# Output projection of three blocks inside the hand-ordered phase, a second column order, and delayed transposes

## The chip, the cores and the metric

The kernel runs on one core of one Trainium2 chip. The metric is device time in microseconds, the median of several executions of the same program. Engines are named as the profile names them: PE is TensorE's matmul side and PEld its weight loads, DVE is VectorE, ACT is ScalarE, POOL is GpSimd, and SP is SyncE, which issues all DMAs here.

## What is computed

One decoder layer on 2048 rows of 1024 columns, in float32. The rows are normed and multiplied by one input matrix. Its columns feed two groups of heads: eight heads of a delta-rule recurrence (RWKV-7) and four of a gated linear attention (GLA). Their outputs side by side, `mix`, go through one output matrix and are added to the input; a SwiGLU FFN and a last norm follow.

```python
n = rms_norm(h, rms1_g[l])
z = n @ w_in[l]
y_rwkv = rwkv7_mixer(z[..., :D_RWKV_IN], ...)
y_gla = gla_mixer(z[..., D_RWKV_IN:], ...)
mix = jnp.concatenate([y_rwkv, y_gla], axis=-1)
h = h + mix @ w_out[l]
n = rms_norm(h, rms2_g[l])
h = h + (silu(n @ ffn_gate[l]) * (n @ ffn_up[l])) @ ffn_down[l]
return rms_norm(h, final_g)
```

## The kernel before

Large products are done with three matmuls each: both operands are split into a high part (a cast on ACT) and a low part (a subtraction on DVE or POOL), and high x high, high x low and low x high are summed in one PSUM bank.

**Phase A** (`phase_a`, lines 326 to 388) computes the input product and the mixers in four blocks of 512 rows. Its instructions are put in order by `Order` (lines 66 to 242). Each `stream` is a generator that issues instructions and yields; `Order.run` keeps a modelled time for each and always resumes the earliest. A stream may yield nothing, the name of an event that it waits for, or a `set`, a `lock` or an `unlock`. A stream that is marked as filler is resumed when the modelled PE has less than 400 ns of work ahead. What comes out is a fixed order on each engine; an instruction whose input is late holds up all behind it on its engine.

The streams (`streams`, line 412):

- `zmm` (597), the filler: 26 columns of 128 outputs per block in the order SEQZ, 24 matmuls each, into banks zd0 and zd1 in turn. Its input tiles "nh" and "nl" (four each) hold the normed rows of a block.
- `weights` (569) loads each column's weights through two buffers "w_raw", casts them on ACT and subtracts on POOL, two columns ahead. `evac` (625) takes the columns out of the banks. `rows` (496) and `prep_a` (534) make the next block's nh and nl, with transposes on PE; two of eight use the bank "mg" and its lock.
- `stage_a` (797), `stage_a2` (938) and `stage_b` (1034) handle pairs of heads ("head" below), 16 in turn. `stage_a2` inverts a triangular system in a loop on POOL (966 to 971), transposes it twice on DVE (984, 986), and then PE runs zt (994) and more, up to wtp (1027). `stage_b` runs the recurrence in eight steps, norms the result on DVE (1092 to 1095), transposes it on PE (ytp, 1102) and stores it to `mix` in DRAM (1119).
- `gmix` (1123), the GLA heads: norm on DVE (1200), then the transpose gotp (1205) on PE, with "mg" locked.

**Phase B** (`phase_b`, 1251) is ordered by the framework, which fills the engines' free places with it while phase A ends. It splits the output matrix (1295), and for each of 16 row tiles loads `mix` and the residual, does 2 x 24 matmuls of 512 columns (1315 to 1317), adds, squares and stores `hs` (1318 to 1321). `prep` (1263) reads hs back, scales and transposes it for the FFN. Then comes the FFN in two halves of 1024 rows (1329 on).

Tiles of phase B take the buffers of phase A by lists of tags (`SEQ`, 1220, and `bt`, 1235): each call takes the next tag of its list. The list "raw" is bk (one buffer), br, br (four buffers); row tiles, residual tiles, the tiles of `prep` and raw FFN weights all draw from it.

Of the kernel before, what the change touches and what calls it, by code (L numbers as in the profile page):

```python
# [20 lines left out]
D = 1024  # L21
# [3 lines left out]
BLK = 512  # L25
# [40 lines left out]
class Order:  # L66
# [126 lines left out]
    def run(self, streams):  # L193

        q = [[0.0, n, name, gen, filler] for n, (name, gen, filler) in enumerate(streams)]
        waiting = {}
        while q:
            pe = self.free.get("PE", 0.0)
            s = min(q, key=lambda s: (max(s[0], pe - self.AHEAD) if s[4] else s[0], s[1]))
            q.remove(s)  # L200
            try:
                r = next(s[3])
            except StopIteration:
                self.take()
# [36 lines left out]
        assert not waiting, waiting.keys()  # L241
        self.check()
# [24 lines left out]
class K:  # L267
# [15 lines left out]

    def rsqrt(self, x, n, name):

        nc = self.nc
        y = self.small.tile([128, n], F32, name=name + "_y")
        t = self.small.tile([128, n], F32, name=name + "_t")
        nc.vector.tensor_scalar(out=y.bitcast(I32), in0=x.bitcast(I32), scalar1=-0.5, scalar2=float(0x5F3759DF),
                                op0=ALU.mult, op1=ALU.add)  # L290
# [4 lines left out]
        return y  # L295


    S2 = -0.5 ** (1 / 3)
# [27 lines left out]
    def phase_a(self, ctx):  # L326
        tc, nc, I = self.tc, self.nc, self.I
        self.ca = ca = ctx.enter_context(tc.tile_pool(name="ca", bufs=1))
        self.s = ctx.enter_context(tc.tile_pool(name="s", bufs=2))
        self.pp = ctx.enter_context(tc.tile_pool(name="pp", bufs=1, space=PSUM))  # L330
        self.x0 = []
        for k in range(KT):
            x = self.s.tile([128, NPR, 128], F32, name="xk", **self.X0[k])
# [56 lines left out]
    def stacks(self):  # L390
        nc = self.nc

        def stack(name, n, order):
# [15 lines left out]
    SEQZ = [ZL, ZK, ZR, ZV, ZQ, ZKG, ZVG, ZK + 1, ZR + 1, ZV + 1, ZVG + 1, ZG, ZOG, ZK + 2, ZR + 2, ZV + 2, ZOG + 1,  # L409
            ZQ + 1, ZKG + 1, ZK + 3, ZR + 3, ZV + 3, ZVG + 2, ZVG + 3, ZOG + 2, ZOG + 3]  # L410

    def streams(self):
        nb = self.T // BLK
        def each(f, m):
            for b in range(nb):
                for i in range(m):
                    yield from f(b, i)
        return [("b", each(self.stage_b, HP), False), ("a2", each(self.stage_a2, HP), False),
                ("e", self.evac(nb), False), ("w", self.weights(nb), False), ("x", self.rows(nb), False), ("p", self.prep_a(nb, 0), False), ("p", self.prep_a(nb, 1), False),
                
                ("a", each(self.stage_a, HP), False), ("g", each(self.gmix, 2), False),
                ("z", self.zmm(nb), True)]
# [146 lines left out]
    def weights(self, nb):  # L569
# [55 lines left out]
    def evac(self, nb):  # L625

        todo = {ZL: self.lora_l, ZG: self.lora_g}
        for b in range(nb):
            for i, ct in enumerate(self.SEQZ):
                if ct == ZQ or ct == ZQ + 1:  # L630
                    yield from self.decay_g(b, ct - ZQ)
                yield f"zm{b}.{i}"
                ps = self.zps.pop((b, i))
                used = ("set", f"ze{b}.{i}")
                if ct == ZL:
                    yield from self.lora_l(b, ps, used)
                elif ct == ZG:
                    yield from self.lora_g(b, ps, used)
                elif ct < ZL:
                    yield from self.rkv_z(b, ct, ps, used)  # L640
                else:
                    yield from self.gla_z(b, ct, ps, used)

    def shift(self, ps, i, rows=128):

# [105 lines left out]
    def gla_z(self, b, ct, ps, used):  # L751
# [32 lines left out]
        else:  # L784
# [7 lines left out]
            self.gla[i, h] = so  # L792
            yield used
            yield ("set", f"go{i}.{h}")


    def stage_a(self, b, hp):
# [140 lines left out]
    def stage_a2(self, b, hp):  # L938
# [95 lines left out]
    def stage_b(self, b, hp):  # L1034
# [11 lines left out]
        for c in range(NCH):  # L1046
# [26 lines left out]
            if c % 4 == 3:  # L1073
# [7 lines left out]
                for x in range(2):  # L1081
# [41 lines left out]
    def gmix(self, b, jj):  # L1123
# [44 lines left out]
        for h in range(2):  # L1168
# [19 lines left out]
            if h:  # L1188
# [46 lines left out]
    def bt(self, cls, name, shape, dtype=F32):  # L1235
        seq = self.SEQ[cls]
        i = self.nb_[cls] = self.nb_.get(cls, -1) + 1
        tag, bufs = seq[i % len(seq)]
        return (self.pp if cls in ("dn", "up") else self.s).tile(shape, dtype, name=name, tag=tag, bufs=bufs)

    def split(self, src, name, cls="W"):
        nc = self.nc
# [8 lines left out]
    def phase_b(self):  # L1251
# [7 lines left out]
        hs = self.dram.tile([T, D], F32, name="hs")  # L1259
        rs, n2 = {}, {}  # L1260
        rsb = self.base.tile([128, T // 128], F32, name="rsb")

# [29 lines left out]
                    n2[nb, k] = (h, l)  # L1292


        wo = [self.split(I["wout"][k * 128:(k + 1) * 128, :], "wo", "W" if k < 6 else "W2") for k in range(KT)]
        steps = [(nb, kp) for nb in range(NB) for kp in range(KT // 2)]
        for t in range(T // 128):
            raw = self.bt("raw", "raw", [128, KT, 128])
            nc.sync.dma_start(out=raw, in_=self.mix[t])
            mh, ml = [], []  # L1300
            for i in range(2):
# [2 lines left out]
                ml.append(self.bt("hid", "ml", [128, 4, 128], F32R))  # L1304
                nc.scalar.copy(out=mh[i], in_=a)
                nc.vector.tensor_tensor(out=ml[i], in0=a, in1=mh[i].bitcast(F32), op=ALU.subtract)
            h = self.bt("raw", "hx", [128, D])
            nc.sync.dma_start(out=h, in_=I["x"][t * 128:(t + 1) * 128, :])
            ss = self.small.tile([128, 2], F32, name="rn_ss")
            for d in range(2):  # L1310
                ps = self.pp.tile([128, 512], F32, name="op", tag=f"zd{d}", bufs=1)
                ds = slice(d * 512, d * 512 + 512)
                for k in range(KT):
                    a, l = mh[k // 4][:, k % 4, :], ml[k // 4][:, k % 4, :]
                    nc.tensor.matmul(out=ps, lhsT=a, rhs=wo[k][0][:, ds], start=(k == 0), stop=False)  # L1315
                    nc.tensor.matmul(out=ps, lhsT=a, rhs=wo[k][1][:, ds], start=False, stop=False)  # L1316
                    nc.tensor.matmul(out=ps, lhsT=l, rhs=wo[k][0][:, ds], start=False, stop=(k == KT - 1))  # L1317
                nc.vector.tensor_tensor(out=h[:, ds], in0=ps, in1=h[:, ds], op=ALU.add)
                nc.scalar.activation(out=self.bt("act", "sq", [128, 512]), in_=h[:, ds], func=AF.Square,
                                     accum_out=ss[:, d:d + 1])  # L1320
            nc.sync.dma_start(out=hs[t * 128:(t + 1) * 128, :], in_=h)
            rs[t] = self.row_rs(ss, rsb[:, t:t + 1])
# [152 lines left out]
```

## Time and profile before

| | us |
|---|---|
| median of 3 runs | 2888.27 (2887.42 to 2889.42) |
| profiled execution | 2882.94 |
| its span | 2881.1 |
| PE busy | 2736.8 (95%) |
| DVE busy | 1414.5 (49%) |
| ACT busy | 985.9 (34%) |
| POOL busy | 676.2 (23%) |
| DMA, mean over the span | 72 GB/s |

The profile is one execution. Busy time is the time in which an engine works on at least one instruction. The granted clock of PE is given as a share of full speed: 1.0 is 2.4 GHz, 0.5 is 1.2 GHz. Idle time of an engine is put down to what ended it. Phase A ends at about 1228 us, the loop of the output projection at about 1386 us; the rest is the FFN.

### The profile page before, as it was taken

Reading aid. Unit: us, or ns where it says so; the run is one execution under the profiler, and the core shown is the slowest. Engines: PE = TensorE matmul, PEld = TensorE weight load, DVE = VectorE, ACT = ScalarE, POOL = GpSimd, SP = SyncE. Lnnn points to the kernel's source line nnn. Section 1 sums busy time; section 2 is a strip of 40 time slices with the busy share of each in tenths; the row PEclk is TensorE's granted clock in tenths of the full one; section 3 lists DMA queues with packets and bytes.
Section 4 is the critical chain, followed back from the end, with each engine's and each line's share of the span. In section 5 each row is a group of like instructions: output and inputs, shape, how many; then the busy total and the mean of one; then the engine's idle time right before and its main releaser. Section 6 shows DMA issues by size and latency. Waiting matters only on the chain.

```text
span 2881.1 us, 38490 instructions
## 1 busy us (share of the span) xinstructions
PE 2736.8 (95%) x14856; PEld 2203.4 (76%) x14856; DVE 1414.5 (49%) x2938; ACT 985.9 (34%) x1907; POOL 676.2 (23%) x1458
## 2 busy tenths in 40 slices
PE   6898999999989998799999999999999999999998
PEld 4777777777767776588788888888878888888886
DVE  5466667676666665644333333333373333333334
ACT  7455554665555554333211111111151111111112
POOL 3666466556654665100000000000000000000000
PEclk9999999999999998799999999999999999999999
DMA  4122212231122111355411111111161111111111
GB/s 141 59 69 65 92 63 63 63 103 62 57 63 60 59 59 37 121 179 179 132 51 44 44 45 58 44 44 44 51 212 51 52 52 52 52 44 44 44 44 59
DMA packets 109641, 206.06 MB, mean 72 GB/s; under 512 B 9104, under 2 KB 50800, under 8 KB 109456
## 3 DMA queue, kind: packets, MB, share of 16 engines
q1 hardware_dynamic: 109456, 203.59, 22.4%
q8 instruction: 117, 1.92, 0.3%
q14 instruction: 68, 0.56, 0.1%
HBM read 178.39 MB, written 25.17 MB: 71 GB/s over the span
## 4 chain that ended last, share of the span: by engine, by line
PE 77%; DVE 9%; POOL 5%; ACT 4%; issue 3%; DMA 1%; SPq 0%; DVEq 0%; POOLq 0%; ACTq 0%
PE ups L1346 6%; PE ups L1348 6%; PE ups L1347 6%; PE dn L1369 6%; PE gps L1346 6%; PE dn L1368 6%; PE gps L1348 6%; PE gps L1347 5%; PE dn L1370 5%; PE zd L615 4%; PE zd L617 3%; PE zd L616 3%; PE op L1315 2%; PE op L1316 2%; PE op L1317 2%
## 5 line engine op out<-in xcount | busy, mean ns | idle before, releaser
L615 PE MATMUL zd<-nh,w_hi 128*128 128x512 f32 x832 | 360.3, 433 | 3.7 <-DVE k L657 2.0
L617 PE MATMUL zd<-nh,w_lo 128*128 128x512 f32 x832 | 333.8, 401 | 3.3 <-POOL w_lo L592 3.3
L616 PE MATMUL zd<-nl,w_hi 128*128 128x512 f32 x832 | 331.7, 399 | 1.2 <-DVE nl L562 1.2
L592 POOL TENSOR_TENSOR w_lo<-w_raw,w_hi 128x512 fp32r<-128x512 f32 x208 | 279.5, 1346 | 220.6 <-ACT w_hi L590 174.9
L1371 DVE TENSOR_TENSOR h<-dn,h 128x512 f32<-128x512 f32 x352 | 242.9, 690 | 179.8 <-PE dn L1370 179.7
L1369 PE MATMUL dn<-wdl,hh 128*128 128x512 f32 x704 | 278.6, 396 | 0.0
L1368 PE MATMUL dn<-wdh,hh 128*128 128x512 f32 x704 | 277.6, 395 | 0.0
L1370 PE MATMUL dn<-wdh,hl 128*128 128x512 f32 x704 | 277.0, 393 | 0.0
L1346 PE MATMUL ups<-n2h,wuh 128*128 128x512 f32 x660 | 260.4, 395 | 0.0
L1347 PE MATMUL ups<-n2l,wuh 128*128 128x512 f32 x660 | 260.4, 395 | 0.0
L1348 PE MATMUL ups<-n2h,wul 128*128 128x512 f32 x660 | 260.0, 394 | 0.0
L1347 PE MATMUL gps<-n2l,wgh 128*128 128x512 f32 x660 | 259.9, 394 | 0.0
L1346 PE MATMUL gps<-n2h,wgh 128*128 128x512 f32 x660 | 259.9, 394 | 0.0
L1348 PE MATMUL gps<-n2h,wgl 128*128 128x512 f32 x660 | 259.3, 393 | 0.0
L1351 DVE TENSOR_TENSOR sgu<-sgu,ups 128x512 f32<-128x512 f32 x88 | 60.2, 685 | 395.0 <-PE ups L1348 393.5
L1247 ACT CAST wdh<-raw 128x1024 fp32r<-128x1024 f32 x44 | 46.3, 1052 | 465.3 <-PE dn L1370 250.3
L617 PEld LDWEIGHTS zd<-nh,w_lo 128*128 128x128 f32 x832 | 159.7, 192 | 42.6 <-POOL w_lo L592 5.8
L615 PEld LDWEIGHTS zd<-nh,w_hi 128*128 128x128 f32 x832 | 160.7, 193 | 36.1 <-issue 5.1
L971 POOL TENSOR_TENSOR lm<-lm,lt 128x60 f32<-128x60 f32 (+24 forms) x496 | 174.6, 352 | 38.8
L616 PEld LDWEIGHTS zd<-nl,w_hi 128*128 128x128 f32 x832 | 161.2, 194 | 27.0 <-DVE nl L562 2.1
L969 POOL TENSOR_TENSOR lt<-lm,ln 128x60 f32<-128x60 f32 (+24 forms) x496 | 161.9, 326 | 38.1 <-DVE ln L953 13.8
L1350 ACT ACTIVATE sgu<-gps 128x512 f32<-128x512 f32 x88 | 52.7, 599 | 344.7 <-PE gps L1348 344.7
(265 smaller groups left out, 4967.7 us busy)
## 6 DMA issues: line engine op xcount, KB each, us to landing
w_raw<-in_win SPq DMA_DIRECT2D x208, 256.0 KB, 2.6
raw<-in_wg SPq DMA_DIRECT2D x44, 512.0 KB, 4.1
raw<-in_wu SPq DMA_DIRECT2D x44, 512.0 KB, 3.6
raw<-in_wd SPq DMA_DIRECT2D x44, 512.0 KB, 3.5
xk<-in_x SPq DMA_DIRECT2D x32, 256.0 KB, 3.3
hx<-in_x SPq DMA_DIRECT2D x16, 512.0 KB, 4.3
raw<-mix SPq DMA_DIRECT2D x16, 512.0 KB, 3.5
hs<-hx SPq DMA_DIRECT2D x16, 512.0 KB, 2.9
```

The source lines that it names most:

```text
L592: nc.gpsimd.tensor_tensor(out=wlo[:, ks, :], in0=raw, in1=whi[:, ks, :].bitcast(F32), op=ALU.subtract)
L615: nc.tensor.matmul(out=ps, lhsT=whi[:, k, :], rhs=nh, start=(k == 0), stop=False)
L616: nc.tensor.matmul(out=ps, lhsT=whi[:, k, :], rhs=nl, start=False, stop=False)
L617: nc.tensor.matmul(out=ps, lhsT=wlo[:, k, :], rhs=nh, start=False, stop=(k == KT - 1))
L971: nc.gpsimd.tensor_tensor(out=lm[:, 0:j, i0:], in0=lm[:, 0:j, i0:], in1=lt[:, 0:j, i0:], op=ALU.add)
L1346: nc.tensor.matmul(out=ps, lhsT=w[0][:, ks], rhs=h, start=(k == 0), stop=False)
L1347: nc.tensor.matmul(out=ps, lhsT=w[0][:, ks], rhs=l, start=False, stop=False)
L1348: nc.tensor.matmul(out=ps, lhsT=w[1][:, ks], rhs=h, start=False, stop=(k == KT - 1))
L1368: nc.tensor.matmul(out=ps, lhsT=hh[:, ts], rhs=wd[f][0][:, ds], start=(f == 0), stop=False)
L1369: nc.tensor.matmul(out=ps, lhsT=hh[:, ts], rhs=wd[f][1][:, ds], start=False, stop=False)
L1370: nc.tensor.matmul(out=ps, lhsT=hl[:, ts], rhs=wd[f][0][:, ds], start=False, stop=(f == 1))
L1371: nc.vector.tensor_tensor(out=H[t][:, ds], in0=ps, in1=H[t][:, ds], op=ALU.add)
```

## The change

The output projection of the first three blocks (row tiles 0 to 11) leaves phase B and becomes filler in phase A after the last column of z. It runs over the 12 tiles for columns 0 to 511 and then again for columns 512 to 1023, 24 groups in all: `out_w` loads the output matrix in 8 slices for each half, into the tiles nh and nl that z has finished with; `out_m` loads and splits rows of `mix`; `out_mm` does the matmuls into zd0 and zd1; `out_e` adds the residual, squares and stores. Phase B keeps tiles 12 to 15, takes the second half of the matrix from phase A and loads the first half again; the reciprocal roots of tiles 0 to 11 are computed together, and two steps of `prep` follow each tile. In the last block z's columns have another order, SEQL. The planned place of zt is 1.5 us later than before, that of ytp and of gotp 2.5 us.

```diff
@@ -208,6 +208,9 @@
             if r is None:
                 q.append(s)
+            elif isinstance(r, float):
+                s[0] += r
+                q.append(s)
...
+    SEQL = [ZL, ZK, ZR, ZV, ZQ, ZKG, ZVG, ZK + 1, ZR + 1, ZV + 1, ZVG + 1, ZK + 2, ZR + 2, ZV + 2, ZG, ZOG,
+            ZK + 3, ZR + 3, ZV + 3, ZOG + 1, ZQ + 1, ZKG + 1, ZVG + 2, ZVG + 3, ZOG + 2, ZOG + 3]
...
-                ("z", self.zmm(nb), True)]
+                ("ow", self.out_w(nb), False), ("om", self.out_m(nb), False), ("oe", self.out_e(nb), False),
+                ("z", itertools.chain(self.zmm(nb), self.out_mm(nb)), True)]
...
-            for i, ct in enumerate(self.SEQZ):
+            for i, ct in enumerate(self.SEQL if b == nb - 1 else self.SEQZ):
...
+    def out_w(self, nb):
+        nc, b = self.nc, nb - 1
+        yield f"w{b}.{NZ - 1}"
+        self.wo = {}
+        for d in range(2):
+            for k in range(KT):
+                raw = self.s.tile([128, 512], F32, name="wo_raw", tag="w_raw", bufs=2)
+                nc.sync.dma_start(out=raw, in_=self.I["wout"][k * 128:(k + 1) * 128, 512 * d:512 * d + 512])
+                yield
+                if not k % 2:
+                    yield f"ok{k // 2}" if d else f"zk{b}.{k // 2}"
+                    pair = [self.s.tile([128, 2, BLK], F32R, name="wo", tag=t, bufs=4) for t in ("nh", "nl")]
+                h, l = [t[:, k % 2] for t in pair]
+                nc.scalar.copy(out=h, in_=raw)
+                yield
+                eng = nc.vector if k % 2 else nc.gpsimd
+                eng.tensor_tensor(out=l, in0=raw, in1=h.bitcast(F32), op=ALU.subtract)
+                self.wo[d, k] = h, l
+                yield ("set", f"wo{d}.{k}")
+    def out_m(self, nb):
...
+        for n in range(2 * (nb - 1) * NPR):
+            t = n % ((nb - 1) * NPR)
...
+                raw = self.s.tile([128, 4, 128], F32, name="mraw", tag="xb", bufs=4)
+                nc.sync.dma_start(out=raw, in_=self.mix[t][:, 4 * i:4 * i + 4, :])
...
+            yield f"zm{nb - 1}.{NZ - 1}"
+            if n > 1:
+                yield f"om{n - 2}"
+            mh, ml = [self.s.tile([128, KT, 128], F32R, name=m, tag=g, bufs=2) for m, g in (("mh", "w_hi"), ("ml", "w_lo"))]
...
+    def out_mm(self, nb):
...
+            yield f"oe{n - 2}" if n > 1 else f"ze{nb - 1}.{NZ - 2 + n}"
+            ps = self.zd("op", [128, 512], n)
+            for k in range(KT):
+                yield f"wo{n // nt}.{k}"
...
+                if k % 2:
+                    yield ("set", f"ok{k // 2}") if n == nt - 1 else None
...
+    def out_e(self, nb):
...
+            h = self.s.tile([128, 512], F32, name="hx", tag="tz", bufs=3)
+            nc.sync.dma_start(out=h, in_=self.I["x"][r, c])
+            yield f"om{n}"
+            nc.vector.tensor_tensor(out=h, in0=self.ops.pop(n), in1=h, op=ALU.add)
+            yield ("set", f"oe{n}")
+            nc.scalar.activation(out=junk, in_=h, func=AF.Square, accum_out=self.ssb[:, t, d:d + 1])
+            yield
+            nc.sync.dma_start(out=self.hs[r, c], in_=h)
...
         nc.vector.transpose(out=W.rearrange("p a k -> p (a k)"), in_=ui.rearrange("p a k -> p (a k)"))
-        yield
+        yield 1500.0
...
-        yield
+        yield 2500.0
         yield f"g{b}"
         ytp = self.pt("yp", "ytp", [128, BLK])
...
-            yield
+            yield 2500.0
             otp = self.mg("gotp", [128, BLK])
...
-        "W": [("nh", 4)] * 4 + [("nl", 4)] * 4 + [("w_hi", 2)] * 2 + [("w_lo", 2)] * 2 + [("gV", 1)],
-        "W2": [("gV", 1), ("e", 1), ("gss", 1), ("br", 4)],
+        "W": [("w_hi", 2)] * 2 + [("w_lo", 2)] * 2 + [("nh", 4)] * 4 + [("nl", 4)] * 4 + [("gV", 1)],
+        "W2": [("gV", 1), ("ln", 1), ("gss", 1), ("e", 1), ("br", 4), ("ar", 2), ("br", 4), ("R", 2)],
+        "op": [("zd0", 1), ("zd1", 1)],
...
-        wo = [self.split(I["wout"][k * 128:(k + 1) * 128, :], "wo", "W" if k < 6 else "W2") for k in range(KT)]
+        wo = [[], [self.wo[1, k] for k in range(KT)]]
+        for k in range(KT):
+            raw = self.bt("raw", "wo_raw", [128, 512])
+            nc.sync.dma_start(out=raw, in_=I["wout"][k * 128:(k + 1) * 128, 0:512])
...
-        for t in range(T // 128):
+        nt = T // 128 - NPR
+        s1, s2 = self.ssb[:, 0:nt, 0], self.ssb[:, 0:nt, 1]
...
+        self.newton(s1, rsb[:, 0:nt], s2)
...
+        for t in range(nt, T // 128):
             raw = self.bt("raw", "raw", [128, KT, 128])
...
             h = self.bt("raw", "hx", [128, D])
...
-            for d in range(2):
+            for d in (1, 0):
...
-            if steps and t > steps[0][0] * 4 + 4:
-                nb, kp = steps.pop(0)
+            for nb, kp in steps[:2]:
                 prep(0, nb, [kp])
+            steps = steps[2:]
```

## Rows read from the trace of the kernel before

**Rows 1.** The page: busy tenths and granted clock of PE, 40 slices of 72 us.

```profile
PE   6898999999989998799999999999999999999998
PEclk9999999999999998799999999999999999999999
```

**Rows 2.** Stretches: start:end length, busy us (count) of PE PEld DVE ACT POOL, clock, DMA.

```profile
50.00:1127.00 1077.00, 997.54 (x7180) 800.03 (x7180) 692.74 (x1646) 584.87 (x1216) 640.01 (x1362) 0.97 0.21 65
1127.00:1190.00 63.00, 37.72 (x246) 27.36 (x247) 37.31 (x94) 24.22 (x45) 21.82 (x64) 0.58 0.32 95
1190.00:1228.00 38.00, 37.57 (x204) 28.85 (x203) 21.80 (x72) 13.68 (x34) 0.00 (x0) 0.98 0.41 134
...
1386.00:1400.00 14.00, 9.82 (x34) 6.54 (x33) 5.56 (x13) 6.44 (x8) 0.00 (x0) 0.88 0.73 240
```

**Rows 3.** PE's waits, 50 to 1127 us, longest first: total us, times, longest us.

```profile
PE ytp L1102 <- DVE y L1095: 14.5, 9, 3.7
PE ch L1065 <- DVE uv L1060: 11.2, 15, 2.1
PE gotp L1205 <- DVE gon L1200: 10.0, 6, 3.2
PE zt L994 <- DVE W L986: 8.4, 7, 4.7
```

**Rows 4.** Timeline of PE: start, us, line, tiles; in brackets idle before and releaser.

```profile
260.73 0.63 PE L1102 MATMUL ytp<-ident,y 128*128 128x128 f32 x4 [0.68 <-DVE y L1095]
...
854.74 1.09 PE L1205 MATMUL gotp<-ident,gon 128*128 128x128 f32 x4 [3.25 <-DVE gon L1200]
...
904.15 0.66 PE L1102 MATMUL ytp<-ident,y 128*128 128x128 f32 x4 [1.90 <-DVE y L1095]
```

**Rows 5.** A stretch of 5 us after the last of these; columns as rows 2.

```profile
905.00:910.00 5.00, 5.00 (x15) 3.56 (x14) 3.78 (x6) 3.49 (x6) 0.00 (x0) 0.66 0.23 79
```

**Rows 6.** Timeline: end of a head's solve on PE, start of the next on ACT.

```profile
1057.82 0.60 PE L1027 MATMUL wtp<-ident,R 128*128 128x128 f32 x4
...
1063.11 2.62 ACT L950 COPY ed<-e 32x256 f32<-32x256 f32 x4
```

**Rows 7.** Groups by line: shapes, count | busy us, mean ns | idle before.

```profile
L592 POOL TENSOR_TENSOR w_lo<-w_raw,w_hi 128x512 fp32r<-128x512 f32 x208 | 279.5, 1346 | 220.6 <-ACT w_hi L590 174.9 <-PE zd L617 14.7 <-issue 12.8
...
L590 ACT CAST w_hi<-w_raw 128x512 fp32r<-128x512 f32 x208 | 125.8, 615 | 12.1 <-DMA w_raw<-in_win 10.8 <-issue 0.8
...
L1247 ACT CAST wgh<-raw 128x1024 fp32r<-128x1024 f32 x44 | 46.2, 1050 | 88.5 <-PE ups L1348 79.6 <-DMA raw<-in_wg 5.5 <-PE op L1317 3.4
...
L1306 DVE TENSOR_TENSOR ml<-raw,mh 128x512 fp32r<-128x512 f32 x32 | 21.6, 688 | 17.6 <-ACT mh L1305 17.4
```

**Rows 8.** DMA issues: count, KB of each, median us from issue to landing.

```profile
w_raw<-in_win SPq DMA_DIRECT2D x208, 256.0 KB, 2.6
raw<-in_wg SPq DMA_DIRECT2D x44, 512.0 KB, 4.1
...
raw<-mix SPq DMA_DIRECT2D x16, 512.0 KB, 3.5
hs<-hx SPq DMA_DIRECT2D x16, 512.0 KB, 2.9
```

**Rows 9.** A stretch inside the FFN, every matmul 512 columns; columns as rows 2.

```profile
1450.00:1500.00 50.00, 50.00 (x217) 40.47 (x216) 15.53 (x19) 8.63 (x12) 0.00 (x0) 1.00 0.15 42
```

**Rows 10.** Timeline of PE at the first FFN weights.

```profile
1396.77 0.80 PE L1346 MATMUL ups<-n,wuh 128*128 128x512 f32 x1 [2.96 <-ACT wuh L1247]
```

**Rows 11.** Timeline of DVE and of POOL where two operations meet.

```profile
959.17 1.65 DVE L1095 TENSOR_TENSOR y<-y,gn_y 128x512 f32<-128x512 f32 x1
...
958.98 1.30 POOL L592 TENSOR_TENSOR w_lo<-w_raw,w_hi 128x512 fp32r<-128x512 f32 x1
```

**Rows 12.** Timeline of PE: last z matmul, and the last head's transposes.

```profile
1126.11 0.40 PE L617 MATMUL zd<-nh,w_lo 128*128 128x512 f32 x1
...
1225.77 0.63 PE L1102 MATMUL ytp<-ident,y 128*128 128x128 f32 x4 [0.17 <-DVE rsb L314]
```

More of the change, by code (lines that the diff above doesn't have):

```diff
@@ new lines, in out_m @@
+    def out_m(self, nb):
+        nc = self.nc
+        self.mt = {}
+        for k in (KT - 2, KT - 1):
+            yield f"pt{nb - 1}.{k}"
+        for n in range(2 * (nb - 1) * NPR):
+            t = n % ((nb - 1) * NPR)
+            b = t // NPR
+            yield f"b{b * HP + HP - 1}"
+            yield f"gh{2 * b + 1}.1"
+            raws = []
+            for i in range(2):
+                raw = self.s.tile([128, 4, 128], F32, name="mraw", tag="xb", bufs=4)
+                nc.sync.dma_start(out=raw, in_=self.mix[t][:, 4 * i:4 * i + 4, :])
+                raws.append(raw)
+            yield
[3 more added lines that the diff above has]
+            mh, ml = [self.s.tile([128, KT, 128], F32R, name=m, tag=g, bufs=2) for m, g in (("mh", "w_hi"), ("ml", "w_lo"))]
+            for i in range(2):
+                ks = slice(4 * i, 4 * i + 4)
+                nc.scalar.copy(out=mh[:, ks], in_=raws[i])
+                yield
+                nc.vector.tensor_tensor(out=ml[:, ks], in0=raws[i], in1=mh[:, ks].bitcast(F32), op=ALU.subtract)
+            self.mt[n] = mh, ml
+            yield ("set", f"mt{n}")
@@ new lines, in out_mm @@
+    def out_mm(self, nb):
+        nc = self.nc
+        self.ops = {}
+        nt = (nb - 1) * NPR
+        for n in range(2 * nt):
+            yield f"mt{n}"
+            yield f"oe{n - 2}" if n > 1 else f"ze{nb - 1}.{NZ - 2 + n}"
+            mh, ml = self.mt.pop(n)
+            ps = self.zd("op", [128, 512], n)
+            for k in range(KT):
+                yield f"wo{n // nt}.{k}"
+                wh, wl = self.wo[n // nt, k]
+                nc.tensor.matmul(out=ps, lhsT=mh[:, k], rhs=wh, start=(k == 0), stop=False)
+                nc.tensor.matmul(out=ps, lhsT=mh[:, k], rhs=wl, start=False, stop=False)
+                nc.tensor.matmul(out=ps, lhsT=ml[:, k], rhs=wh, start=False, stop=(k == KT - 1))
+                if k % 2:
+                    yield ("set", f"ok{k // 2}") if n == nt - 1 else None
+            self.ops[n] = ps
+            yield ("set", f"om{n}")
@@ new lines, in out_e @@
+    def out_e(self, nb):
+        nc = self.nc
+        nt = (nb - 1) * NPR
+        yield "evac"
+        junk = self.s.tile([128, BLK], F32, name="osq", tag="sh", bufs=1)
+        for n in range(2 * nt):
+            d, t = n // nt, n % nt
+            r = slice(t * 128, t * 128 + 128)
+            c = slice(d * 512, d * 512 + 512)
+            h = self.s.tile([128, 512], F32, name="hx", tag="tz", bufs=3)
[4 more added lines that the diff above has]
+            nc.scalar.activation(out=junk, in_=h, func=AF.Square, accum_out=self.ssb[:, t, d:d + 1])
+            yield
+            nc.sync.dma_start(out=self.hs[r, c], in_=h)
+            yield
@@ L1258, in phase_b @@
         nc.sync.dma_start(out=g2, in_=I["g2"])
[L1259 removed]
+        hs = self.hs
         rs, n2 = {}, {}
@@ L1292, in prep @@
                     n2[nb, k] = (h, l)
-        wo = [self.split(I["wout"][k * 128:(k + 1) * 128, :], "wo", "W" if k < 6 else "W2") for k in range(KT)]
-        steps = [(nb, kp) for nb in range(NB) for kp in range(KT // 2)]
-        for t in range(T // 128):
+        wo = [[], [self.wo[1, k] for k in range(KT)]]
+        for k in range(KT):
+            raw = self.bt("raw", "wo_raw", [128, 512])
+            nc.sync.dma_start(out=raw, in_=I["wout"][k * 128:(k + 1) * 128, 0:512])
+            if not k % 2:
+                pair = [self.bt("W2", "wo", [128, 2, 512], F32R) for _ in range(2)]
+            h, l = [t[:, k % 2] for t in pair]
+            nc.scalar.copy(out=h, in_=raw)
+            nc.vector.tensor_tensor(out=l, in0=raw, in1=h.bitcast(F32), op=ALU.subtract)
+            wo[0].append((h, l))
+        steps = [(nb, kp) for nb in range(NB) for kp in range(KT // 2)]
+        nt = T // 128 - NPR
+        s1, s2 = self.ssb[:, 0:nt, 0], self.ssb[:, 0:nt, 1]
+        nc.vector.tensor_tensor(out=s1, in0=s1, in1=s2, op=ALU.add)
+        nc.vector.tensor_scalar(out=s1, in0=s1, scalar1=1.0 / D, scalar2=RMS_EPS, op0=ALU.mult, op1=ALU.add)
+        self.newton(s1, rsb[:, 0:nt], s2)
+        for t in range(nt):
+            rs[t] = rsb[:, t:t + 1]
+        for t in range(nt, T // 128):
             raw = self.bt("raw", "raw", [128, KT, 128])
@@ L1306, in phase_b @@
                 nc.vector.tensor_tensor(out=ml[i], in0=a, in1=mh[i].bitcast(F32), op=ALU.subtract)
+            ts = slice(t * 128, (t + 1) * 128)
             h = self.bt("raw", "hx", [128, D])
-            nc.sync.dma_start(out=h, in_=I["x"][t * 128:(t + 1) * 128, :])
-            ss = self.small.tile([128, 2], F32, name="rn_ss")
-            for d in range(2):
-                ps = self.pp.tile([128, 512], F32, name="op", tag=f"zd{d}", bufs=1)
-                ds = slice(d * 512, d * 512 + 512)
+            nc.sync.dma_start(out=h, in_=I["x"][ts, :])
@@ L1313, in phase_b @@
+            for d in (1, 0):
+                ps = self.bt("op", "op", [128, 512])
+                dd = slice(d * 512, d * 512 + 512)
                 for k in range(KT):
                     a, l = mh[k // 4][:, k % 4, :], ml[k // 4][:, k % 4, :]
-                    nc.tensor.matmul(out=ps, lhsT=a, rhs=wo[k][0][:, ds], start=(k == 0), stop=False)
-                    nc.tensor.matmul(out=ps, lhsT=a, rhs=wo[k][1][:, ds], start=False, stop=False)
-                    nc.tensor.matmul(out=ps, lhsT=l, rhs=wo[k][0][:, ds], start=False, stop=(k == KT - 1))
@@ L1318, in phase_b @@
[L1318 to L1322, printed above, removed]
-            if steps and t > steps[0][0] * 4 + 4:
-                nb, kp = steps.pop(0)
+                    wh, wl = wo[d][k]
@@ new lines, in phase_b @@
+                    nc.tensor.matmul(out=ps, lhsT=a, rhs=wh, start=(k == 0), stop=False)
+                    nc.tensor.matmul(out=ps, lhsT=a, rhs=wl, start=False, stop=False)
+                    nc.tensor.matmul(out=ps, lhsT=l, rhs=wh, start=False, stop=(k == KT - 1))
+                nc.vector.tensor_tensor(out=h[:, dd], in0=ps, in1=h[:, dd], op=ALU.add)
+                nc.scalar.activation(out=self.bt("act", "sq", [128, 512]), in_=h[:, dd], func=AF.Square,
+                                     accum_out=self.ssb[:, t, d:d + 1])
```

15 lines of the change are left out of this document (11 added, 4 removed).

## Prediction

> **What bounds the kernel now.** I read the page first, then the table of stretches, then the waits of PE (TensorE), then single rows of the timeline. The digits of the page show a PE that is full from about 1230 us on and has holes before [rows 1]. The stretches give the sizes [rows 2]. From 50 to 1127 us PE is busy 997.5 of 1077 us at a mean clock of 0.97, so it loses 79.5 us idle and about 30 us to the clock. From 1127 to 1190 us it is busy only 37.7 of 63 us, at 0.58, which is nearly all at the lower of the two levels (0.5 is 1.2 GHz, 1.0 is 2.4 GHz). The last z matmul starts at 1126.1, and the last head's output transposes come at 1225.8 [rows 12]: between them runs the serial chain of the last two heads with no z left to fill PE. From 1386 to 1400 us PE waits for the first FFN weights, 4.2 us idle. So PE bounds the program, and what can be won is its holes. The FFN after 1400 us has the same work before and after, and I book nothing there.
>
> The tail, from the last z matmul to a full FFN, loses before: 25.3 idle + 37.7 x 0.42 = 15.8 by the clock (1127 to 1190), 0.4 + 0.8 (1190 to 1228), 4.2 + 1.2 (1386 to 1400), together **47.7 us** [rows 2].
>
> **The change, part by part.**
>
> *PE work.* Of 16 row tiles, 12 move into the hand-ordered phase, in 24 groups of 24 matmuls: 576. At 217 matmuls in 50 us [rows 9] one takes 0.230 us, so 132.7 us of PE work leave the later loop and the same 132.7 us are added as filler. None is saved; only holes can be.
>
> *Filler against chain.* After the last z, PE has 37.7 x 0.58 = 22 us of chain work (at full clock) and 132.7 us of filler, while the chain took 99.7 us [rows 12]. The filler so outlasts the last head by some 70 to 80 us. A later last head costs nothing until that cover is gone; that is also why the new column order (heads 2 and 3 three columns earlier) is booked at 0. Heads are not waiting for their columns: the triangular solve of one head starts only when that of the head before has ended (wtp at 1057.8, next ed at 1063.1 [rows 6]). Bounds -3 to +3 us.
>
> *What the tail loses after.* (a) Start: the weights of the filler come in 8 slices through two raw buffers, and each pair of slices waits until the last z column has read the old tile. A cycle of two slices is a landing of 2.6 [rows 8] + cast 0.62 + subtraction on POOL (GpSimd) 1.35 [rows 7] + about 0.2 = 4.8 us, against 1.4 us that PE needs for them. Four cycles end 13.5 us after the last z instead of 5.5, 8 us idle, half of it filled by the chain: 4 (bounds 0 to 13). (b) PE waits of the chain inside the filler, over some 85 us: at the rate of 1190 to 1228 us 2.7, at that of 50 to 1127 us 8.6; I take 5. (c) At the twelfth group the weights change to the other 512 columns, again slice by slice into tiles that the twelfth group just read: 8 us idle and 1 of clock, 9. By then the chain is about over and fills nothing. Bounds 0 (chain late enough to fill it) to 20 (no slice fetched ahead, 8 x 4.8 less 5.5 and more). (d) The first late tile needs a buffer of the filler's last residual store (landing 2.9 [rows 8]): 2, bounds 0 to 3. (e) In the late loop the 8 weight slices, the row tiles and the residual tiles draw from one list of three tags, one of them with a single buffer. Counting the draws, the residual of tile 12 and the row tile of tile 13 both get that single buffer. So tile 13 can't be loaded before tile 12 is stored: drain 0.25 + add 0.69 + store 2.9 + load 3.5 + cast 0.62 + issue 0.4 = 8.4 [rows 7, 8], and 1 for a lower clock, 9.5, bounds 0 to 12. (f) The other tags hold two of four buffers as weights, so later loads are tight: 2, bounds 0 to 6. (g) The first FFN weight draws the same single buffer after the residual of tile 15: 0.25 + 0.69 + 2.9 + 4.1 + cast 1.05 + issue 0.5 = 9.5 [rows 7, 8], and 1 of clock: 10.5, bounds 4 to 14; before it was 5.4, its longest part the 2.96 us of [rows 10]. Sum 4 + 5 + 9 + 2 + 9.5 + 2 + 10.5 = **42**. The tail gains 47.7 - 42 = 6 us; with all low ends it gains 41, with all high ends it loses 29.
>
> *Queues.* Per group SP (SyncE, all DMAs) issues two row loads, a residual load and a store, 1 MB in 5.5 us. A store waits in SP's order for its sum, and the next group's loads stand behind it; two groups of row buffers are ahead, so I book 0 (bounds 0 to 3, in b). ACT gets two casts and a square, DVE two subtractions and a sum per group, some 2 us each of 5.5, booked in b. The small reciprocal roots of 12 tiles are now done at once: 0.
>
> *A rule that speaks against it.* The DVE multiply at 959.2 took 1.65 us while POOL ran a subtraction from 959.0 to 960.3 [rows 11], against 0.69 for another two-operand op of that size [rows 7]. The Trainium skill (SBUF — State Buffer, section "SBUF: two separate sides") calls the port pair of the two engines an exclusive lock that blocks the loser for the whole instruction. The trace agrees in that row. By the rule each of the 8 slices that now go to POOL could hold up a DVE subtraction for 1.35 us, 10.8 in all, about half of it in (a) and (c); the gain below would then be some 13 instead of 18.
>
> *Delayed transposes.* The three waits they aim at are 14.5 + 10.0 + 8.4 = 32.9 us of PE idle in 22 cases [rows 3]. Five of these, 12.1 us, lie where a block ends (first 0.68 at 260.7, last 3.25 at 854.7 [rows 4]); there the next block's z isn't ready, and PE has nothing to do instead. 20.8 us in 17 cases can be filled with z. The 1.90 us at 904.2 [rows 4] is followed by a clock of 0.66 over 5 us [rows 5], 1.7 us lost; I estimate three such places, 5 us. I take 60% of both, 15.5, since the order is a plan and the longest wait (4.7) is beyond its delay; bounds 0 to 26. Against it: the bank "mg" is held 2.5 us longer, and two of eight transposes for the next block need it: 0 to 7.5 over three block ends, I take 3.5. The solve chain gets 1.5 us longer per head and has no slack [rows 6]; where PE was waiting there anyway this costs nothing. Net **12**.
>
> Sum 6 + 12 = 18. On the profiled execution's 2882.9 (span 2881.1) that is 2864.9; the median of the runs is 5.3 higher, so 2888.3 - 18 = **2870**.
>
> **The rivals.** *Holes covered* (18 + c, e and half of g): PE gets the chain's rest in the switch, and tile 13 and the FFN weight find their buffers free. For it: before, PE was full in the same loop [rows 1]. Against: the counted draws. Gain 18 + 9 + 9.5 + 5 = 41, 2847. *Nothing comes of it:* the delayed ops leave PE waiting on the next op in the fixed order (the ch waits of 11.2 us [rows 3] are not touched), so the 12 fall to 0 to 3, and the tail gives 6 or less: 2885. *The solve sets the pace* (slower): each head's solve starts 2 to 6 us after the one before ends [rows 6], POOL, ACT and DVE stand in fixed orders behind it, and z can run no more than two heads ahead, because their buffers are freed by it. If that chain and not PE paces 50 to 1127 us, the delay is added 16 times: 16 x 1.5 = 24, and 7.5 at the block ends, less 8.4 of zt waits and the 6 of the tail: +17, 2905. It decides from the point where z waits for the heads; today z isn't among the four longest sums of waits [rows 3], which speaks against it.
>
> **How the numbers follow.** Forecast (2860 to 2880) 0.47; holes covered 0.18; nothing 0.15; solve 0.20. Faster by over 0.2% (5.8 us, about what a measurement of this kernel can tell from no change) is the forecast less its upper end, 0.44, and 0.18: 0.62. Same 0.15 + 0.03 = 0.18. Slower 0.20. The range takes in most of the covered case and of the solve case, half of each being left out (0.19): 2845 to 2905.
>
> **What would show it.** In the profile after: the waits of ytp, gotp and zt before the last z should fall from 32.9 to some 20 us, and the stretch to the last z should be about 12 us shorter (if it is longer, the solve rival holds); the 60 us after the last z should run at a clock near 1.0; PE should have holes at the change of the weights, before tile 13 (about 8 us, waiting for a cast behind a load) and before the first FFN matmul (about 10). The prediction is wrong if these holes are absent (then too high) or if the first part grows.

## The result and the profile after

| | before | after |
|---|---|---|
| median of 4 runs each, us | 2887.85 | 2932.97 |
| lowest to highest, us | 2887.28 to 2889.42 | 2931.81 to 2937.36 |
| profiled execution, us (its span) | 2882.9 (2881.1) | 2932.1 (2930.3) |

The change is slower: the ratio after to before is 1.0158, interval 1.0141 to 1.0176, that is 45 us. The two profiles are 49 us apart, as the one of before is 5 us faster than its median. The forecast was 18 us faster with a range of 2845 to 2905; the result lies outside it and on the other side.

The page of after, busy tenths and granted clock of PE in 40 slices of 73 us ([rows 1]):

```profile
PE   5999899899999998987699999999999999999998
PEclk9899999999999998988899999999999999999999
```

Before, both rows had a 7 in the slice from 1152 us. Now the slices from 1099 and 1172 us hold an 8 and a 9: the stretch behind the last z is mostly filled. But 8, 7 and 6 stand in the three slices from 1245 us on, right before the FFN. Stretches of after, columns as in [rows 2]: to the last z, the filler, two parts of the filler, and the late loop (tiles 12 to 15 to the first FFN matmul):

```profile
50.00:1112.00 1062.00, 984.58 (x7045) 791.05 (x7043) 682.43 (x1604) 582.64 (x1207) 631.07 (x1354) 0.97 0.22 67
1112.00:1336.00 224.00, 192.23 (x1042) 148.47 (x1042) 108.93 (x254) 83.07 (x183) 33.82 (x81) 0.89 0.47 151
...
1150.00:1180.00 30.00, 22.11 (x88) 16.72 (x87) 12.73 (x34) 7.98 (x19) 14.77 (x45) 0.72 0.32 102
1244.00:1280.00 36.00, 21.87 (x57) 13.35 (x56) 14.16 (x31) 10.01 (x22) 3.81 (x3) 0.67 0.41 132
...
1336.00:1439.20 103.20, 63.54 (x257) 49.31 (x256) 35.57 (x98) 28.68 (x58) 0.00 (x0) 0.79 0.41 137
```

For the ledger I cut each span into stretches of 10 us and summed the idle time of PE and busy x (1 - clock). One profile of each kernel:

| us lost, idle + clock | 50 us to last z | last z to FFN (before: no filler) | filler | late loop | first FFN matmul at |
|---|---|---|---|---|---|
| before | 79.4 + 28.1 | 26.2 + 16.1 = 42.3 | | | 1387.0 |
| after | 77.4 + 25.2 | 98.4 | 31.8 + 17.2 = 49.0 | 39.7 + 10.7 = 50.4 | 1439.2 |

The FFN itself takes 1494 us before and 1491 after. So the 52 us up to the first FFN matmul hold the whole difference: 56 more are lost behind the last z and 5 fewer ahead of it, while PE's busy time at full clock differs by 1 us (filler and late loop were cut into their own stretches, so their sum is 1 off the tail's). The 5 fewer can't be told from chance: five later kernels (e3, e5, e6, e10, e12) run the same instructions of phase A ahead of the last z, and their profiles lose 106 to 113 us there, against 103 in after and 107.5 before. Half of the tail's loss is the late loop. Its waits (engine, tile, releaser: us in total, times, longest):

```profile
PE tcn L1382 <- DVE hk L1377: 19.4, 3, 7.5
PE gps L1465 <- ACT wgh L1349: 6.3, 1, 6.3
PE op L1434 <- ACT mh L1423: 5.8, 3, 4.1
PE tcn L1382 <- DVE rsb L316: 4.7, 1, 4.7
```

The timeline of SP around tile 14 (start, time, line, transfer), and that of PE (in brackets the idle time and what ended it):

```profile
1372.66 0.32 SPq L1440 DMA_DIRECT2D hs<-hx  x1
1375.31 0.37 SPq L1371 DMA_DIRECT2D hk<-hs  x1
1381.38 0.32 SPq L1417 DMA_DIRECT2D raw<-mix  x1
1384.01 0.37 SPq L1371 DMA_DIRECT2D hk<-hs  x1
```

```profile
1379.36 1.94 PE L1382 MATMUL tcn<-ident,hk 128*128 128x128 f32 x8 [7.46 <-DVE hk L1377]
1382.01 1.97 PE L1382 MATMUL tcn<-ident,hk 128*128 128x128 f32 x8 [0.71 <-DVE n2l L1392]
1385.27 0.80 PE L1434 MATMUL op<-wo,mh 128*128 128x512 f32 x1 [1.28 <-ACT mh L1423]
```

Each load is issued 2.6 to 6.1 us after the transfer before it: SP has nothing else to do, each load waits for a tile. The hk block of 1375.31 holds rows stored long ago (rows 0 to 1023, all in the filler). By the draws of the list its tile is the one that held tile 13's residual, which is free only when the store of 1372.66 has landed. The same tile then goes to tile 14's rows: they are asked for at 1381.38, right when the transposes at 1379.36 (1.94 us) have read the hk block.

Inside the filler two holes stand out. The first: DVE, then POOL, then PE.

```profile
1160.29 0.29 DVE L1161 TENSOR_TENSOR uv<-yp,R 64x128 f32<-64x128 f32 x1 [5.68 <-PE yp L1156]
1167.53 0.69 DVE L1405 TENSOR_TENSOR wo<-wo_raw,wo 128x512 fp32r<-128x512 f32 x1 [6.94 <-POOL lt L1070]
```

```profile
1167.29 0.20 POOL L1070 TENSOR_TENSOR lt<-lm,ln 128x8 f32<-128x8 f32 x1
```

```profile
1175.64 0.77 PE L1156 MATMUL yp<-S,ar 128*128 128x128 f32 x2 [6.73 <-DVE y L1184]
```

L1405 is phase B's: it makes the low half of the first late weight slice and writes it into tag ln, which the last head's solve on POOL still reads, for the last time at 1167.29. DVE takes its queue in order, so it stands 6.94 us, and the recurrence of the head before, whose steps come next on DVE, lets PE stand 6.73 us at 1175.64. In the profiles of e3, e6 and e12, which leave this as it is, DVE stands there 10.4 to 10.9 us. The second hole is the change of the weights, 1244 to 1280, 14.1 idle and 7.1 by the clock. PE's two largest sums of waits in the filler, and then the longest wait at the change of the weights, on PE, ACT and SP:

```profile
PE op L870 <- ACT wo L823: 13.3, 5, 4.6
PE yp L1156 <- DVE y L1184: 6.7, 1, 6.7
```

```profile
1264.05 0.80 PE L870 MATMUL op<-wo,mh 128*128 128x512 f32 x1 [4.62 <-ACT wo L823]
```

```profile
1263.38 1.37 ACT L823 CAST wo<-wo_raw 128x512 fp32r<-128x512 f32 x2 [8.62 <-DMA wo_raw<-in_wout]
```

```profile
1259.63 0.38 SPq L1220 DMA_DIRECT2D mix<-y  x1
1260.10 0.95 SPq L817 DMA_DIRECT2D wo_raw<-in_wout  x2
```

The third pair of slices is asked for at 1260.10, right behind the last head's store, though the two raw tiles had been read at about 1256.

### The profile page after: what moved, and what is told of

Read it like the earlier page. It is cut to its first block, busy times and chain, and to the rows that moved or that the text cites. A ratio compares the mean times of both kernels' runs of the same rounds, so it can differ in the third digit from the quotient of the medians.

```text
span 2930.3 us, 38668 instructions
## 1 busy us (share of the span) xinstructions
PE 2745.3 (94%) x14856; PEld 2207.3 (75%) x14856; DVE 1419.1 (48%) x2874; ACT 1006.5 (34%) x1947; POOL 679.2 (23%) x1466
## 4 chain that ended last, share of the span: by engine, by line
PE 57%; DVE 4%; DMA 3%; ACT 1%; POOL 1%; issue 1%; SPq 0%; DVEq 0%; ACTq 0%; POOLq 0%
PE gps L1465 6%; PE gps L1467 6%; PE ups L1465 6%; PE ups L1467 6%; PE gps L1466 6%; PE ups L1466 6%; PE dn L1488 5%; PE dn L1487 5%; PE dn L1489 5%; DMA wo_raw<-in_wout 1%; DMA hx<-in_x 1%; PE op L870 1%; PE op L871 1%; PE op L1434 1%; PE op L872 1%
```

## Experiments

All ratios are to the kernel before on the same chip, with their intervals; in us they are taken on 2888. The changed kernel stands at 1.0158. Where an expectation gives 13.4 us lost to the clock in the late loop, it took the mean clock of the whole loop; by stretches of 10 us it is 10.7.

### The delays alone, and the change without them

```diff
 (kernel before)
-        yield            # after W in stage_a2; before ytp; before gotp
+        yield 1500.0     # 2500.0 before ytp and gotp
```

> The kernel before with one thing of the change: the three groups of transposes are delayed (1.5, 2.5, 2.5 us) in the planned order; no filler, old column order. Theory A, from the trace after: the holes only moved. The three waits fall from 32.9 us to 8.4, but waits of the recurrence (ch, yp) rise from about 17 to 41 us, so the gain is 0 to 4 us: 2884 to 2888. Rival B, the prediction's term: 12 us, 2876. Rival C, the solve sets the pace: +8 to +20, 2896 to 2908. The trace tells A from B by the sum of all waits of PE between 50 us and the last z: unchanged within 4 us (A) or 12 us less (B).

Measured: 0.9958 (0.9942 to 0.9974), 12 us faster. The size is B's, the prediction's; the road is A's. PE's waits from 50 to 1112 us, and the two stretches to the last z and to the FFN:

```profile
PE ch L1068 <- DVE uv L1063: 21.2, 20, 3.3
PE yp L1058 <- DVE S L1074: 16.1, 14, 3.8
...
PE ytp L1105 <- DVE y L1098: 3.6, 2, 1.9
```

```profile
50.00:1108.50 1058.50, 981.37 (x7086) 789.68 (x7085) 680.05 (x1616) 581.84 (x1206) 632.67 (x1362) 0.97 0.20 66
1108.50:1373.80 265.30, 240.12 (x1251) 189.87 (x1250) 137.64 (x391) 91.40 (x198) 21.82 (x64) 0.90 0.42 144
```

The aimed-at waits fall from 32.9 us [rows 3] to 3.6, but ch rises from 11.2 to 21.2 and yp to 16.1, so the idle time to the FFN falls by only 3.2 us (105.6 to 102.4). The FFN starts 13.2 us earlier. The clock gives 2.3; the other 7.7 are busy time that the same work no longer takes. That fits operations that now run among z matmuls and overlap with them instead of standing alone, but a few records can be missing from a trace, so this part is inferred.

> The changed kernel without the delays (the three plain waiting points back). Theory A: within 4 us of the changed kernel's 2933, as the delays only moved holes. Rival B: some 12 us slower, 2945. Rival C: 8 to 20 us faster, 2913 to 2925, as each head's solve starts earlier and the last head ends earlier in the filler.

Measured: 1.0143 (1.0125 to 1.0160), against the change 4 us less, within what can be told. Here A holds: in the whole change the delays are worth nothing that can be measured.

### The column order

```diff
-  enumerate(self.SEQL if b == nb - 1 else self.SEQZ)   # e4: changed kernel
+  enumerate(self.SEQZ)                                 # e8: the reverse, in the kernel before
```

> The kernel before with one thing of the change: the other column order in the last block, no filler, no delays. Theory N, the order itself costs: the last head's columns are the same but the GLA columns come later, and the last heads end about as late as without it or later; 5 to 15 us slower than before, 2893 to 2903. Rival O, it costs only together with the filler and its prefetched weights (DVE's blocked queue): within 4 us of 2888. Rival P, it helps alone, as it was arranged for: 3 to 10 us faster.

Measured: 1.0006 (0.9996 to 1.0017): O, alone it is worth nothing, as the prediction booked.

> The changed kernel with the old column order in the last block. Theory G: the order in itself is worth nothing, as the prediction booked (within 3 us of 2933). Rival H: the new order gives the chain work earlier and so lets the last head end earlier in the filler; without it the chain ends later, which fills the change of the weights at the twelfth group (21 us lost between 1244 and 1280): 5 to 15 us faster, 2918 to 2928. Rival I: without it PE has less to do in the 60 us after the last z: 5 to 15 us slower, 2938 to 2948.

Measured: 1.0094 (1.0077 to 1.0111), 18 us less than the change: H's size. The last head's transposes end at 1236.1 instead of 1256.6, and the filler loses 20.6 + 10.9 us instead of 31.8 + 17.2. But H's reason is wrong: the change of the weights still loses 17.4 us (10.7 + 6.7 in 1225 to 1260). Most of what is gone are holes ahead of it, 16 us: DVE's wait for ln is shorter, 3.8 us, and PE's waits for yp<-y (6.7 us) and ytp (4.8 us) aren't there (waits of DVE and of PE in the filler):

```profile
DVE wo L1405 <- POOL lt L1070: 3.8, 1, 3.8
```

```profile
PE op L870 <- ACT wo L823: 9.8, 5, 4.2
PE ch L1166 <- DVE uv L1161: 3.7, 1, 3.7
```

### The late loop

```diff
-  "W2": [gV, ln, gss, e, br, ar, br, R]
+  "W2": [gV, ln, gss, e, ar, ar, R, R]     # e3: two more br free for loads
```

> The changed kernel with one list of tile tags altered: two of the eight tiles that hold the output weights' first 512 columns move from tag br (4 buffers) to the second buffers of ar and R, so all four br buffers are free for the late loop's loads. Theory D, starvation of buffers: in the late loop of 4 tiles (1336 to 1439 us, 39.7 us idle and 13.4 us lost to the clock) the loads of row tiles, residuals and hk blocks share 3 buffers, of which the first n2 tile takes one more; with two more free the loop loses 20 to 35 us less: 2898 to 2913. Rival E, latency: the hk loads stand behind the store of the tile's own sum on SP, and PE has only the next tile as cover, so the holes stay: within 5 us of 2933. Theory F, the prediction's own: only the two places with the single-buffer tag bk cost, and these stay: 2 to 5 us less, 2928 to 2931.

Measured: 1.0053 (1.0040 to 1.0066), 30 us less. D, at its upper half; E and F fall. The late loop loses 20.3 + 3.2 us instead of 39.7 + 10.7, and the hk waits are down from 19.4 to 2.1 us. What is left is mostly the wait for the first FFN weight:

```profile
PE gps L1465 <- ACT wgh L1349: 10.8, 1, 10.8
...
PE tcn L1382 <- DVE hk L1377: 2.1, 1, 2.1
```

To see whether the rest is latency, the loop got tiles of its own:

```diff
 (e3's list, and)
-  raw, hx, hk: all from the list bk, br, br
+  raw, hx of tiles 13, 14: w_hi, w_lo;  of 12, 15: bk, br;  hk: br
-  for nb, kp in steps[:2]: prep(0, nb, [kp])
+  for nb, kp in steps[:3]: prep(0, nb, [kp])     # none left after tile 15
+  self.nb_["raw"] += 1                           # first FFN weight in bk
```

> The changed kernel with only the late loop mended: weights of the first 512 columns off br, row tiles and residuals of tiles 13 and 14 in w_hi and w_lo, hk blocks in br, tile 15's row tile and the first FFN weight in bk, three prepared blocks behind each tile; new order, delays, the late subtraction into ln and two raw tiles at the change of weights stay. Theory D in full: all of the late loop's 53 us (39.7 idle, 13.4 clock) come from loads that wait for tiles, so 45 to 53 us less than 2933: ratio 0.9975 to 1.0005. Rival E in its smaller form: past the 28 us that two more br buffers gave, latency remains: ratio 1.003 to 1.006.

Measured: 0.9969 (0.9957 to 0.9982), 55 us less than the change, and 9 us faster than the kernel before; in the profiles the loop is 46 us shorter. D in full, but not by tiles alone: of the 55, e3's two tiles are 30, and the other 25 are tiles and the third block behind each row tile together, which no run takes apart in this kernel (e11 below does it in another, 10 us). The late loop in this kernel, as a stretch and as PE's waits:

```profile
1333.20:1390.40 57.20, 54.34 (x257) 43.28 (x257) 34.17 (x89) 27.76 (x57) 0.00 (x0) 0.97 0.57 194
```

```profile
PE op L1437 <- DVE ml L1425: 2.2, 1, 2.2
PE op L1435 <- ACT mh L1424: 0.6, 1, 0.6
```

It lasts 57 us instead of 103, and no wait for hk, for a row tile past the first, or for an FFN weight is left.

### The two holes in the filler

```diff
-  "W2": [gV, ln, gss, e, br, ar, br, R]
+  "W2": [gV, gss, e, ln, br, ar, br, R]     # e5: first low half not into ln
```

> The changed kernel with one list of tags in another order: the low half of the first pair of late weight slices goes to tag gss instead of ln. Theory J, a blocked queue: on DVE the subtraction of a late weight slice stands 6.9 us (1160.6 to 1167.5) until the last head's solve on POOL has read the tile ln for the last time, and the recurrence of the head before, whose steps stand behind it on DVE, makes PE wait 6.7 us at 1175.6; the stretch 1150 to 1180 loses 7.9 us idle and 6.2 to the clock. Without that wait 7 to 14 us less than 2933: 2919 to 2926. Rival K: the chain is late anyway and the holes go to its next wait: within 4 us of 2933.

Measured: 1.0117 (1.0099 to 1.0135), 12 us less: J. DVE no longer waits for POOL there, and the filler loses 23.0 + 10.5 us instead of 31.8 + 17.2. PE's waits for yp and for the weights in it:

```profile
PE op L870 <- ACT wo L823: 12.4, 4, 4.1
...
PE yp L1156 <- DVE y L1184: 1.9, 1, 1.9
```

```diff
-  raw = tile(tag="w_raw", bufs=2)
+  raw = tile(tag=[w_raw, w_raw, w_dup, w_iup][k % 4 if d else k % 2])   # e6
```

> The changed kernel with four instead of two tiles for the raw slices of the other 512 columns of the output weights, at the change of the weights. Theory L: the change costs 14.1 us idle and 7.2 to the clock (1244 to 1280 us) because each pair of slices is loaded only after the pair before it was cast; with four tiles 8 to 15 us less: 2918 to 2925. Rival M: the loads are late for another reason (they stand behind the last head's store on SP), or the casts and subtractions set the pace: within 5 us of 2933.

Measured: 1.0119 (1.0105 to 1.0133), 11 us less: L, in the lower half. The loads are now ahead of the last head's store on SP, and the wait for the casts falls from 13.3 to 3.7 us (PE's wait, then SP):

```profile
PE op L871 <- ACT wo L824: 3.7, 3, 1.7
```

```profile
1252.80 5.61 SPq L818 DMA_DIRECT2D wo_raw<-in_wout  x4
1263.79 0.38 SPq L1221 DMA_DIRECT2D mix<-y  x1
```

So M is partly right as well: two raw tiles were costly because their next loads came to stand behind that store.

### Together

e7 is e4, e5's idea (W2: gV, gss, e, ln, ar, ar, R, R), e6 and the late loop's own tiles, with steps[:2] as in the change.

> The changed kernel with its four suspected costs taken away together: old column order, tag ln last among the weights' tiles, four raw tiles at the change of the weights, and a late loop with tiles of its own (row tiles and residuals of tiles 13 and 14 in w_hi and w_lo, hk blocks in four br, tile 15's row tile in bk, first FFN weight in bk). If the costs add: 18 (old order) + 30 (buffers) + 7 to 14 + 8 to 15 = 63 to 77 less than 2933, 2856 to 2870, faster than the kernel before with delays alone (2876). If they share holes (the chain that ends earlier no longer covers the next stretch): 2875 to 2890.

Measured: 0.9927 (0.9914 to 0.9939), 67 us less than the change and 21 faster than before. The parts don't simply add. Singly they gave 18 + 12 + 11 and, for the loop, 30 (e3) or 55 (e12), 71 or 96 in all; e7's loop lies between those of e3 and e12, and e11, which has e12's whole loop, reaches 77. The order and the wait for ln share holes (e4, e10). In the next two runs one thing each was put back:

> The kernel with the four costs taken away (2868, ratio 0.9927) without the delays. Theory Q: the delays are worth 12 us where the stretch behind the last z doesn't swallow them, so without them 8 to 14 us slower, ratio 0.9955 to 0.9975 (2875 to 2881). Rival R: with a filler behind the last z the delays are worth nothing, because the last heads' chain ends later by them (within 4 us, ratio 0.9913 to 0.9941).

Measured: 0.9966 (0.9954 to 0.9979), 11 us slower: Q. With the old order and the four costs away the delays pay.

> The kernel with the four costs taken away (2868, ratio 0.9927) with the new column order in the last block. Theory S: the order costs because it makes the last solve on POOL later, and the prefetched weights' subtraction on DVE waits for that; with that wait gone it costs 0 to 6 us (ratio 0.9927 to 0.9948). Rival T: the order costs its 18 us by itself through the later chain: ratio 0.998 to 1.000.

Measured: 0.9936 (0.9921 to 0.9950), 3 us slower, which can't be told from nothing: S. The order costs little once no weight slice waits for the last solve and the change of the weights has four raw tiles. The last run adds the third block behind each late row tile:

> The kernel with the four costs taken away (2868, ratio 0.9927), with three instead of two blocks of normalized rows prepared behind each late row tile, so none is left behind the last one and the br buffers come free for the first FFN weights earlier. There PE waited 4.9 us at 1380.95 for the second weight's cast, whose load was issued only at 1370.65. If that load comes earlier: 4 to 7 us less, 2861 to 2864, ratio 0.990 to 0.9915. If the hk blocks now wait on the stores: 0 to 5 us slower.

Measured: 0.9893 (0.9875 to 0.9911), 10 us less than e7: more than expected. The FFN took 1498.9 us in e7's profile and 1492.1 here; the rest, 4.5 us, was won ahead of it. This version beats both kernels: 2858.6 against 2888.

## Why the prediction failed, point by point

Two terms of the sum turned its sign: (f), the buffers of the late loop, booked at 2 us and worth some 20 us of idle time and 7 by the clock, and the column order, booked at 0 and worth 18.

- *PE bounds, 132.7 us of filler are moved and none is saved.* Right: busy time at full clock up to the FFN differs by 1 us, and the FFN is the same.
- *Delayed transposes, 12.* Right in size where nothing takes it back (e1: 12, e9: 11), wrong in the working: I let 60% of three waits vanish, while the chain simply waited at its next operations. The gain came mostly as less busy time. In the change itself it was lost (e2), and why stays open. The later solve may meet the weight slice in ln: DVE waits 4.6 us there in e2, and 6.9 to 10.9 with the delays (after, e3, e6, e12). Or the new order leaves the delays less to win: with the old order the last z starts at 1126.1 and 1130.1 us without them (before, e9) and at 1108.5 to 1117.2 with them (e1, e4, e7, e11), with the new one at 1114.1 and 1119.7 without (e8, e2) and at 1111.8 to 1118.7 with (after, e3, e5, e6, e10, e12). No run takes the two apart.
- *Column order, 0.* Right alone (e8), wrong here: 18 us (e4). "A later last head costs nothing until that cover is gone" is the sentence that failed. The cover was there, as long as booked: the last head's transposes end at 1256.6, the filler at 1336. But PE takes filler and chain in one fixed order, so a chain that is late stops the filler too; cover works only where the order has filler to give at that place. With the wait for ln, the change of the weights and the late loop mended, the order costs only 3 us (e10).
- *(a) and (b), 4 + 5.* With the old order the filler ahead of the change of the weights loses 10.0 us (7.4 + 2.6, stretches 1111 to 1225 of e4), close to the 9 booked. In the change it is 26.0 (16.6 + 9.4, 1112 to 1244). The step that is missing is a wait: phase B's loads, casts and subtractions slip into the engines' queues while phase A ends, and their tiles are taken over from heads still at work. I asked that question of SP, and of ACT and DVE only their busy time. 12 us (e5).
- *(c) the change of the weights, 9, bounds 0 to 20.* Measured 21.2, of it 14.1 idle. The cycle of 4.8 us was right, but "8 x 4.8 less 5.5" is 32.9 and not 20; a cycle serves two slices, so it should have been 4 x 4.8 less 5.5, 13.7, which is what PE idled. I let the first two slices come free, put the clock at 1, and didn't see the last head's store on SP ahead of the third pair. Two more raw tiles buy back 11 (e6).
- *(d) to (g), 24.* The term that turned the sign: measured 50.4, and 55 us of time (e12). The draws of (e) and (g) are there as counted: tile 13's rows are asked for 3.0 us after tile 12's store (1352.32, 1355.30), and the first FFN weight only after tile 15's (1425.80, 1432.79). In idle time (d) is 2.6, (e) 5.6 and (g) 11.0 (4.7 for the last hk block and 6.3 for the weight), together 19 where 22 were booked, of it 2 of clock. The mis-sized one is (f), 2 with bounds 0 to 6: PE idles 9.5 us before tile 14 and 10.9 before tile 15, and some 7 of the 10.7 us of clock are lost behind these two holes. I counted the tags at two places and not through the loop. Of five tiles in the list two hold weights, and from the first prepared block on a third holds a normalized block, which leaves one br and bk for 8 hk blocks, 4 row tiles and 4 residuals; and all 8 hk blocks, spread over eight row tiles before, now fall behind four. The hk waits alone are 19.4 us, and two more tiles cut them to 2.1 (e3).
- *The rule on the port pair* was priced at up to 10.8 us. Such waits are there (below), but only three of the filler's eight subtractions on POOL held a DVE operation up (at 1106.61, 1113.83 and 1250.29, 1.05 to 1.12 us against medians of 0.16 to 0.35), by 2.6 us together. What took 11 us off the change of the weights were tiles (e6), not another engine.
- *The rivals.* "Holes covered" fell, for its holes were the ones that grew. "Nothing comes of it" was right on the delays in the change (e2), not on the tail. "Solve sets the pace" gave the sign but not the road: the last z starts at 1111.8 instead of 1126.1, earlier and not later, of which the order alone gives 12 us (e8).
- *The signs.* The three waits fell to 3.6 us and not to some 20, without the gain that was to come with it. The 60 us after the last z run at a clock of 0.86, not near 1.0. The three holes are there.
- *The range.* Its upper end came from the solve rival; the tail's high ends together give the same (29 lost, 12 won by the delays: 2905). The bounds of (b) were rates of the kernel before, where no late weight slice stands in the chain's queues, and those of (f) rested on no row. Bounds of that kind bound nothing.

## What to carry to other kernels

Before moving work into an earlier phase, walk the list of buffers through every load of the part that is left behind, with all that is held meanwhile, not only at the two places that look tight: here three of five tiles were held. Two more free tiles bought back 30 us, and the loop with tiles of its own and a third block behind each row tile 55, where the whole change was to win 18. An operation placed early in an in-order queue is a wait for whatever last reads its destination tile, and the price is paid by what stands behind it on that engine. Filler covered a late chain here only where the order had filler at that very place.

## What the runs showed of the hardware

A small DVE operation can pay for a POOL subtraction like a large one. The 16 instances of L1193, a TENSOR_SCALAR on 128x8, take 0.17 us in the median; beside a subtraction on POOL one took 1.05 us, ending 0.04 us after that. L301, on the same size, took 1.12 us at 1113.83 and ended 0.02 us after another (timelines of DVE and POOL of after):

```profile
1250.29 1.05 DVE L1193 TENSOR_SCALAR va<-va 128x8 f32<-128x8 f32 x1
1113.83 1.12 DVE L301 SCALAR_TENSOR_TENSOR gn_y<-gn_t,gn_y 128x8 f32<-128x8 f32 x1
1130.75 0.68 DVE L1279 TENSOR_TENSOR gat<-gsc,cst 128x512 f32<-128x512 f32 x1
```

```profile
1250.04 1.26 POOL L826 TENSOR_TENSOR wo<-wo_raw,wo 128x512 fp32r<-128x512 f32 x1 [9.14 <-ACT wo L823]
1113.65 1.28 POOL L826 TENSOR_TENSOR wo<-wo_raw,wo 128x512 fp32r<-128x512 f32 x1 [0.28 <-ACT wo L823]
1130.16 1.27 POOL L826 TENSOR_TENSOR wo<-wo_raw,wo 128x512 fp32r<-128x512 f32 x1 [3.21 <-PE gsc L1277]
```

Not every operation pays: in the third pair L1279, with one input in PSUM (gsc) and one in SBUF, runs wholly beside the subtraction and takes 0.68 us, no more than other operations of that size. The Trainium skill (SBUF — State Buffer, section "SBUF: two separate sides") has the loser of the port pair blocked for the whole instruction of the other, and among DVE operations only those with two SBUF inputs or in a two-port mode compete for the pair. The rows of L301 (two SBUF inputs) and L1279 agree; whether L1193, with one input, ran in such a mode no run shows.

A row of short holes cost more than its idle time. After the hole of 7.46 us the transposes at 1379.36 took 1.94 us for eight, against 1.04 at 1351.40, which no hole preceded; the granted clock from 1380 to 1390 was 0.58, near the lower of its two levels (columns as in [rows 2]), and the late loop lost 10.7 us to the clock on top of 39.7 idle:

```profile
1380.00:1390.00 10.00, 8.01 (x29) 6.13 (x28) 4.82 (x8) 4.68 (x8) 0.00 (x0) 0.58 0.47 159
```
